# Modulation sums on VectorE earlier, and norm 2 turned into matmul operands in another order

## The chip, the cores and the metric

One core of a Trainium2 chip. The metric is the device time of one execution in microseconds. The kernel of before took 2047.05 us (median of three runs, 2043.01 to 2047.86). One more execution was profiled; it took 2050.43 us, of which the profile's span, from the first to the last instruction, is 2048.7 us.

## The reference, cut to what matters

One layer of a diffusion backbone, on 128 context and 128 latent tokens of width 2048, all in float32. A conditioning vector per stream gives six modulation vectors of width 2048; the layer is a mixer and a feed-forward:

```python
mod = silu(c) @ w_mod + b_mod          # 2048 -> 6 * 2048, once for c_ctx and once for c
shift1, scale1, gate1, shift2, scale2, gate2 = split(mod, 6)
h = rmsnorm(x, norm1_g) * (1 + scale1) + shift1
...                                    # h @ w_in, three branches, their projections
x = x + gate1 * (merged @ w_out)
h2 = rmsnorm(x, norm2_g) * (1 + scale2) + shift2
x = x + gate2 * (square(relu(h2 @ w_ff1)) @ w_ff2)
```

The output is a last rmsnorm of x, and the final states of two of the branches.

## The kernel before

**Tiles.** All weights are stored as tiles of 128 x 1024 floats (0.52 MB), called units here. For each unit SP issues a load into a buffer raw; ScalarE rounds it to wh (type fp32r); VectorE subtracts and leaves the rest in wl. The activations are kept in the same two parts: Hh and Hl hold 16 k-tiles of 128 features by 256 tokens. A product of two such numbers is three matmuls: high with high, low weight with high, high weight with low activation. So most units are 24 matmuls of 256 columns or 12 of 512.

**Order.** The program is one list of steps, 674 units long, that run_stream walks in order; it splits up to three units (two more from a second set of buffers in the first part) ahead of the matmuls. All other work (norms, scans, residuals) are generators, the fillers: pump, called between matmuls, lets them add instructions to the engines' queues as long as a planned clock says that VectorE and ScalarE are not too far ahead of TensorE. A filler that must be done is forced by finish. Each engine executes its queue in the order in which this planner wrote it.

**Modulation.** shift1 and scale1 are made on TensorE at the start. gate1, shift2, scale2 and gate2 (chunks 2 to 5) are made on VectorE by mods, the background filler, which is last in the list and runs only when VectorE's planned time is under 0.8 us ahead of TensorE's. A chunk is 32 pieces. A piece is one 128 x 1024 tile of w_mod, loaded into mraw by SP two pieces ahead, and two VectorE instructions that multiply it with the broadcast vector cb (one for each stream) and sum the products into part. quota says from which unit on piece m may run, so that the sums are spread: gate1, shift2 and scale2 are pieces 0 to 95, gate2 is 96 to 127 and waits until the first feed-forward block is through. The marks a to e are unit numbers:

```python
if m < 72:
    return a + (b - a) * m / 72
if m < 96:
    return b + (c - b) * (m - 72) / 24
return d + (e - d) * (m - 96) / 32
```

a is unit 88, b unit 370 (the start of the two last branch projections, 16 units), c is six units before the end of the output projection (unit 412 of 418), d and e lie in the feed-forward.

**Output projection.** 32 units in four parts: 16 for the left half of the columns (part 0), 8 for the next quarter (1), and twice 4 for an eighth each (2 and 3). After each part resid multiplies the result in PSUM with gate1, adds it to x (both on VectorE), and ScalarE squares and sums it. At the start of part 3 stands

```python
call(lambda: (self.drain_mod(3), self.drain_mod(4), self.make_gs(1, 0, 16), ...))
```

where drain_mod forces the background until the chunk is done, and make_gs forms (1 + scale2) * norm2_g.

**Norm 2.** x lies with tokens on the partitions. norm2(0) finishes the residuals, computes 1/rms of each token (rtok) and starts eight generators modulate2, one for each pair of k-tiles: VectorE scales x by 1/rms into a temporary tp, TensorE transposes it into a PSUM bank pf, ScalarE writes scale * pf + shift to Hh, VectorE writes the same in full precision over pf, and subtracts Hh from it to make Hl. The pair that comes first (one=True) does this one k-tile after the other. Each pair is finished one unit before the feed-forward's first block, ff1(0, 0), reads it. There block takes the k-tiles in order; within a k-tile each of the eight column groups gets its three products (high, low weight, low activation) one behind the other, and pump is called after every second group.

Of the kernel before, what the change touches and what calls it, by code (L numbers as in the profile page):

```python
# [7 lines left out]
F32 = mybir.dt.float32  # L8
F32R = mybir.dt.float32r
U8 = mybir.dt.uint8  # L10
AF = mybir.ActivationFunctionType
ALU = mybir.AluOpType
AX = mybir.AxisListType

P = 128
# [16 lines left out]
W = "wait"  # L32
# [162 lines left out]
class Backbone:  # L195
# [255 lines left out]
            elif s["kind"] == "call":  # L451
                s["do"]()

    def block(self, units, nk, xh, xl, evac, orient="B", pre=None):


        nc = self.nc
        st = {}
        steps = []
        per = nk // len(units)  # L460
        cols = NB // per
        nb = max(4 // per, 1)

        def do(u, hi, lo):
            if u == 0:
                if pre is not None:
                    pre()
                st["b"] = [self.psb.tile([P, 512], F32, tag="b", name=self.nm("pb")) for _ in range(nb)]
            if u >= len(units) - 2:
                self.evac = self.t["pe"] + 24 * 0.12 * (len(units) - u)  # L470
            for k in range(u * per, u * per + per):
                off = (k - u * per) * cols
                ah, al = xh(k), xl(k)
                for c in range(2 * cols // min(cols, 512) if orient == "A" else 2 * nb):
                    if orient == "B":
                        o = st["b"][c // 2][:, (c % 2) * 256:(c % 2) * 256 + 256]
                        w = slice(off + c * P, off + c * P + P)
                        ops = ((hi[:, w], ah), (lo[:, w], ah), (hi[:, w], al))
                        first, lastc = c % 2 == 0, c % 2 == 1
                    else:  # L480
                        n = min(cols, 512)
                        z, v = divmod(c * n, cols)
                        o = st["b"][c * n // 512][:, c * n % 512:c * n % 512 + n]
                        w = slice(off + v, off + v + n)
                        t = slice(z * P, z * P + P)
                        ops = ((ah[:, t], hi[:, w]), (ah[:, t], lo[:, w]), (al[:, t], hi[:, w]))
                        first, lastc = c * n % 512 == 0, (c + 1) * n % 512 == 0
                    for j, (a, b) in enumerate(ops):
                        nc.tensor.matmul(o, lhsT=a, rhs=b, start=(k == 0 and j == 0 and first),
                                         stop=(k == nk - 1 and j == 2 and lastc), skip_group_check=True)  # L490
                    if lastc:
                        self.pump()
            if u == len(units) - 1:
                self.evac = np.inf
                evac(st["b"])

        for u in range(len(units)):
            steps.append(dict(kind="mm", unit=units[u], do=lambda hi, lo, u=u: do(u, hi, lo)))
        return steps
# [223 lines left out]
    def quota(self, m):  # L723

        a, b, c, d, e = self.marks
        if m < 72:
            return a + (b - a) * m / 72
        if m < 96:
            return b + (c - b) * (m - 72) / 24
        return d + (e - d) * (m - 96) / 32  # L730

    def mods(self, chs):
# [657 lines left out]
    def run(self):  # L1390
        nc, I = self.nc, self.I
# [4 lines left out]
        hh = lambda k: self.Hh[:, k, :]  # L1396
        hl = lambda k: self.Hl[:, k, :]
# [8 lines left out]
        def win(blk, **kw):  # L1406
            return self.block([I["win"][blk, k] for k in range(16)], 16, hh, hl, **kw)
# [18 lines left out]
        def call(f):  # L1426
            return [dict(kind="call", do=f)]
# [3 lines left out]
        steps = self.start_steps(win(1, evac=act_evac("FF", 1, AF.Sigmoid)),  # L1431
                                 self.block(half(0), 16, hh, hl, act_evac("FB", 2, AF.Sigmoid)))
        A = win(3, evac=act_evac("qA", 3, AF.Silu))
        B = self.block(half(1), 16, hh, hl, act_evac("FB", 2, AF.Sigmoid, 2))
# [4 lines left out]
        count = lambda: sum("unit" in s for s in steps)  # L1439
        marks = [count()]  # L1440
# [16 lines left out]
        for part in range(3):  # L1457
            pre, evac = self.qkv_evac(part)
# [125 lines left out]
        for part, (c, i, c0, _) in enumerate(PIECES):  # L1584
            w = I["wout" + c]
            wo = self.block([w[part - 2 if c == "c" else 0, k] for k in range(w.shape[1])], 16, hh, hl,
                            lambda b, part=part: resid(b, part), orient="A",
                            pre=(lambda: self.finish(*self.resids)) if c == "c" else None)
# [29 lines left out]
        def ff1(g, blk):  # L1618
            def pre():
                if (g, blk - 1) in self.hidgen:  # L1620
                    self.finish(self.hidgen[g, blk - 1])
                if blk == 0:
                    z = (8, 9, 10, 11) if g % 2 == 0 else (0, 1, 2, 3)
                    self.hid[g] = [self.slot(i, [P, 8, 256], F32R) for i in z]

            def square(r):
                hi, lo = self.hid[g][blk], self.hid[g][2 + blk]
                for j in range(4):
                    nc.vector.tensor_tensor(out=r[:, j, :], in0=r[:, j, :], in1=r[:, j, :], op=ALU.mult)
                yield W  # L1630
                for j in range(4):
                    nc.scalar.copy(flat(hi, j), r[:, j, :])
                yield W
                for j in range(4):
                    nc.vector.tensor_tensor(out=flat(lo, j), in0=r[:, j, :], in1=flat(hi, j).bitcast(F32), op=ALU.subtract)

            def evac(b):
                r = self.slot(4 if blk == 0 else 7, [P, 4, 512])
                for j in range(4):
                    nc.scalar.activation(r[:, j, :], b[j], AF.Relu)  # L1640
                self.hidgen[g, blk] = self.add(square(r), first=True)

            steps = self.block([I["wff1"][2 * g + blk, k] for k in range(16)], 16, hh, hl, evac, pre=pre)
            if g == 0 and blk == 0:
                out = [dict(kind="call", do=lambda: norm2(0), hold=True)]
                for k, s in enumerate(steps):
                    out += [s]
                    if k % 2 == 0 and k // 2 + 1 < 8:
                        out += call(lambda c=k // 2 + 1: norm2(c))
                return out  # L1650
            return steps
# [53 lines left out]
            self.fing = self.slot(10, [P, D])  # L1705
            nc.gpsimd.dma_start(self.fing, I["fing"].partition_broadcast(P))

        marks += [count() - 6, count() + 16, count() + 160]
        self.marks = marks
        f1 = ff1(0, 0) + call(lambda: setattr(self, "late", True)) + ff1(0, 1) + ff1(1, 0) + ff1(1, 1)  # L1710
        steps += f1
        steps += ff2(0, 0) + ff2(0, 1) + ff1(2, 0) + ff1(2, 1) + ff2(1, 0) + ff2(1, 1)
# [8 lines left out]
        for s in range(2):  # L1721
            v, f = self.x1[1][:, s, 768:1024], self.fing[:, 1792:2048]
            nc.vector.scalar_tensor_tensor(out=v, in0=v, scalar=r[:, s:s + 1], in1=f, op0=ALU.mult, op1=ALU.mult)
            for i, c, w, dve in ((0, 0, 512, False), (0, 512, 512, True), (1, 0, 768, s == 1)):
                v = self.x1[i][:, s, c:c + w]
# [46 lines left out]
    def modulate2(self, n0, x, r, one=False):  # L1772


        nc = self.nc
        k, h = yield from self.gettmp()
        h2 = h.rearrange("p (a b) -> p a b", a=2)
        i = None
        for js in ((0,), (1,)) if one else ((0, 1),):
            c, n = js[0] * P, len(js) * P  # L1780
            for s in range(2):
                nc.vector.tensor_scalar(out=h[:, 256 * s + c:256 * s + c + n], in0=x[:, s, c:c + n], scalar1=r[:, s:s + 1], scalar2=None, op0=ALU.mult)
            yield W
            if i is None:
                i, b = yield from self.getbank()
            for j in js:
                for s in range(2):
                    nc.tensor.transpose(b[:, 256 * j + s * P:256 * j + s * P + P], h[:, 256 * s + j * P:256 * s + j * P + P], self.ident)
            yield W
            o = [(self.Hh[:, n0 + j, s * P:s * P + P], b[:, 256 * j + s * P:256 * j + s * P + P],  # L1790
                  self.gs[:, 1, n0 + j, s:s + 1], self.modc[:, 3, n0 + j, s:s + 1]) for j in js for s in range(2)]
            for d, v, g, sh in o:
                nc.scalar.activation(d, v, AF.Identity, bias=sh, scale=g)
            for m, (d, v, g, sh) in enumerate(o):
                j, s = js[m // 2], m % 2
                nc.vector.tensor_scalar(out=v, in0=v, scalar1=g, scalar2=sh, op0=ALU.mult, op1=ALU.add)
            yield W
            j = js[0]
            hi, lo = self.Hh[:, n0 + j:n0 + j + len(js), :], self.Hl[:, n0 + j:n0 + j + len(js), :]
            nc.vector.tensor_tensor(out=lo, in0=b[:, 256 * j:256 * j + 256 * len(js)].rearrange("p (a b) -> p a b", a=len(js)),  # L1800
                                    in1=hi.bitcast(F32), op=ALU.subtract)
        self.putbank(i)
        self.puttmp(k)

# [95 lines left out]
```

## Time and profile before

| what | value |
|---|---|
| median of three runs | 2047.05 us |
| profiled execution | 2050.43 us, span 2048.7 us |
| TensorE matmul busy | 1958.6 us, 96% of the span |
| VectorE busy | 1484.5 us, 72% |
| ScalarE busy | 1013.3 us, 49% |
| of VectorE: splits wl | 610 x 1221 ns, 741.6 us |
| of VectorE: modulation sums junk<-mraw,cb | 256 x 1219 ns, 312.2 us |
| loads of mraw | 128 x 512 KB on SP's queue |
| HBM traffic | 224 GB/s over the span |

All rows of the profile bear one line, L171, since a helper records every instruction; so the tiles' names tell the work. pb is a PSUM bank of the main matmuls, pf one of the fillers', wh and wl are the split weights, Hh and Hl the split activations, mraw and junk the modulation sums, tp a temporary, z a large buffer with many uses, modc the modulation vectors, rtv, rtu and rtr the steps of 1/rms. A row gives an engine, an operation, out<-in with shapes, and in brackets the idle time before it and what ended it. The windows' PEclk is the granted TensorE clock, 1.00 being full.

### The profile page before, as it was taken

The numbers are of one execution on the slowest core, as the hardware profiler recorded it, in microseconds if no ns is written. First come the engines' busy times: TensorE is split into PE (matmuls) and PEld (weight loads), VectorE is DVE, ScalarE is ACT, GpSimd is POOL, SyncE is SP. The second block draws the span as 40 slices with busy tenths as digits, with TensorE's granted clock in tenths as the row PEclk, the third lists the DMA queues.
The fourth block names the chain that finished last, engine by engine and source line by source line (L and its number), as shares of the span: only waits on it lengthen the run. The fifth ranks groups of instructions, "written<-read, shape, count | busy, mean of one in ns | idle before, by whom it ended". The sixth has DMA issues, their size and how long they took to land.

```text
span 2048.7 us, 31030 instructions
## 1 busy us (share of the span) xinstructions
PE 1958.6 (96%) x12023; PEld 1727.4 (84%) x12023; DVE 1484.5 (72%) x2128; ACT 1013.3 (49%) x1486; POOL 49.1 (2%) x120
## 2 busy tenths in 40 slices
PE   5999999999999999999999997699999999999997
PEld 3769988999888889888888876599988998998886
DVE  6875797978887998556876878766676676555475
ACT  6774645476645544366434433444444443344343
POOL 0000000000000000110000000000000000000000
PEclk9999999999999999999999998799999999999998
DMA  9876665655567757655687777466667667566663
GB/s 339 312 288 216 206 206 195 217 192 184 178 206 232 261 195 246 216 185 194 232 301 252 256 279 253 158 202 222 225 228 254 217 227 237 191 201 210 208 235 136
DMA packets 124508, 460.55 MB, mean 225 GB/s; under 512 B 14216, under 2 KB 14792, under 8 KB 122184
## 3 DMA queue, kind: packets, MB, share of 16 engines
q1 hardware_dynamic: 116496, 423.96, 61.0%
q0 software_dynamic: 7568, 34.35, 4.9%
q8 instruction: 94, 1.54, 0.3%
q14 instruction: 54, 0.44, 0.1%
q10 hardware_dynamic: 296, 0.26, 0.0%
HBM read 447.97 MB, written 10.53 MB: 224 GB/s over the span
## 4 chain that ended last, share of the span: by engine, by line
PE 56%; DVE 9%; DMA 4%; ACT 2%; issue 2%; POOL 0%; DVEq 0%; ACTq 0%; SPq 0%; POOLq 0%
PE pb L171 53%; PE pf L171 4%; DVE wl L171 3%; DVE z L171 2%; DVE junk L171 1%; DVE m L171 1%; ACT wh L171 1%; DMA raw<-in_win 1%; DMA z<-in_s0gd 1%; DMA raw<-in_wouta 1%; DMA raw<-in_woutb 1%; DMA raw<-in_woutc 0%; DVE pf L171 0%; DMA mraw<-in_wmodr 0%; ACT L171 0%
## 5 line engine op out<-in xcount | busy, mean ns | idle before, releaser
L171 DVE TENSOR_TENSOR wl<-raw,wh 128x1024 fp32r<-128x1024 f32 x610 | 741.6, 1221 | 471.6 <-ACT wh L171 470.9
L171 ACT CAST wh<-raw 128x1024 fp32r<-128x1024 f32 x610 | 637.1, 1048 | 828.4 <-PE pb L171 686.3
L171 PE MATMUL pb<-Hh,wh 128*128 128x256 f32 x1864 | 533.4, 286 | 5.5 <-ACT Hh L171 3.1
L171 PE MATMUL pb<-Hl,wh 128*128 128x256 f32 x1864 | 529.8, 284 | 1.1 <-DVE Hl L171 1.1
L171 PE MATMUL pb<-Hh,wl 128*128 128x256 f32 x1864 | 529.6, 284 | 0.2 <-DVE wl L171 0.2
L171 PE MATMUL pb<-wh,z 128*128 128x512 f32 (+1 forms) x1472 | 444.2, 383 | 3.3 <-ACT z L171 3.3
L171 PEld LDWEIGHTS pb<-Hh,wh 128*128 128x128 f32 x1864 | 358.6, 192 | 8.1 <-ACT Hh L171 3.3
L171 PEld LDWEIGHTS pb<-Hl,wh 128*128 128x128 f32 x1864 | 358.4, 192 | 1.6 <-DVE Hl L171 1.5
L171 PEld LDWEIGHTS pb<-Hh,wl 128*128 128x128 f32 x1864 | 358.7, 192 | 1.1 <-DVE wl L171 0.4
L171 PE MATMUL pb<-wh,Hh 128*128 128x512 f32 (+1 forms) x800 | 317.0, 396 | 24.8 <-ACT wh L171 22.8
L171 PEld LDWEIGHTS pb<-wh,z 128*128 128x128 f32 x1472 | 273.2, 189 | 59.5 <-ACT z L171 4.5
L171 DVE SCALAR_TENSOR_TENSOR junk<-mraw,cb 128x1024 bf16<-128x1024 f32 x256 | 312.2, 1219 | 4.7 <-DMA mraw<-in_wmodr 2.4
L171 PE MATMUL pb<-wl,Hh 128*128 128x512 f32 (+1 forms) x800 | 307.0, 384 | 3.4 <-DVE wl L171 3.4
L171 PE MATMUL pb<-wh,Hl 128*128 128x512 f32 (+1 forms) x800 | 306.4, 383 | 0.0
L171 PE MATMUL pb<-wl,z 128*128 128x512 f32 (+1 forms) x736 | 281.8, 383 | 0.9 <-DVE wl L171 0.9
L171 PEld LDWEIGHTS pb<-wh,Hh 128*128 128x128 f32 x800 | 151.9, 190 | 53.5 <-ACT wh L171 23.7
L171 PEld LDWEIGHTS pb<-wl,Hh 128*128 128x128 f32 x800 | 151.9, 190 | 30.6 <-DVE wl L171 5.3
L171 PEld LDWEIGHTS pb<-wh,Hl 128*128 128x128 f32 x800 | 151.5, 189 | 29.7
L171 PEld LDWEIGHTS pb<-wl,z 128*128 128x128 f32 x736 | 138.5, 188 | 28.8 <-DVE wl L171 1.1
L171 DVE TENSOR_TENSOR z<-z,z 128x512 f32<-128x512 f32 (+4 forms) x120 | 90.8, 788 | 13.2 <-ACT z L171 9.4
L171 DVE SCALAR_TENSOR_TENSOR cy<-z,par,cy 128x258 f32<-128x258 f32 (+1 forms) x192 | 53.7, 332 | 1.9
L171 PEld LDWEIGHTS pf<-m,z 128*128 128x128 f32 x384 | 49.7, 191 | 3.7 <-ACT z L171 0.4
(187 smaller groups left out, 1366.0 us busy)
## 6 DMA issues: line engine op xcount, KB each, us to landing
raw<-in_win SPq DMA_DIRECT2D x249, 512.0 KB, 4.0
raw<-in_wff SPq DMA_DIRECT2D x224, 512.0 KB, 4.3
mraw<-in_wmodr SPq DMA_DIRECT2D x128, 512.0 KB, 5.4
raw<-in_wbr SPq DMA_DIRECT2D x48, 512.0 KB, 4.2
z<-in_wmods SPq DMA_DIRECT2D x39, 512.0 KB, 5.6
raw<-in_wmods SPq DMA_DIRECT2D x25, 512.0 KB, 6.3
cb<-csd POOLq DMA_DIRECT2D x8, 1024.0 KB, 7.7
raw<-in_wouta SPq DMA_DIRECT2D x16, 512.0 KB, 4.5
```

What stands on the lines that cost most here:

```text
L171: return f(*a, **k)
```

## The change

Three edits. (1) In quota 84 pieces instead of 72 are due by b, and the other 12 by c, which is now 24 units before the end of the output projection (unit 394) instead of six. (2) In modulate2 all scalings come first, then all transposes into one bank, then the rest for each k-tile; this holds for the first pair too, which had one chain behind the other. VectorE's full-precision result goes to the temporary instead of back into PSUM, and the subtraction reads it there; the wait before the subtraction falls away for the first pair. (3) In ff1(0, 0) alone (late=True) block issues, for each k-tile, the 16 products with Hh of all eight column groups first, and the 8 with Hl behind them; pump is called among the last 8.

```diff
-    def block(self, units, nk, xh, xl, evac, orient="B", pre=None):
+    def block(self, units, nk, xh, xl, evac, orient="B", pre=None, late=False):
...
+                for c in range(8 if late else 0):
+                    o = st["b"][c // 2][:, (c % 2) * 256:(c % 2) * 256 + 256]
+                    for m, w in enumerate((hi, lo)):
+                        nc.tensor.matmul(o, lhsT=w[:, c * P:c * P + P], rhs=ah, start=(k == 0 and m == 0 and c % 2 == 0),
+                                         stop=False, skip_group_check=True)
...
                     for j, (a, b) in enumerate(ops):
+                        if late and j < 2:
+                            continue
...
-        if m < 72:
-            return a + (b - a) * m / 72
+        if m < 84:
+            return a + (b - a) * m / 84
         if m < 96:
-            return b + (c - b) * (m - 72) / 24
+            return b + (c - b) * (m - 84) / 12
...
-            steps = self.block([I["wff1"][2 * g + blk, k] for k in range(16)], 16, hh, hl, evac, pre=pre)
+            steps = self.block([I["wff1"][2 * g + blk, k] for k in range(16)], 16, hh, hl, evac, pre=pre, late=(g, blk) == (0, 0))
...
-        marks += [count() - 6, count() + 16, count() + 160]
+        marks += [count() - 24, count() + 16, count() + 160]
...
-        for js in ((0,), (1,)) if one else ((0, 1),):
+        parts = ((0,), (1,)) if one else ((0, 1),)
+        for js in parts:
             c, n = js[0] * P, len(js) * P
             for s in range(2):
                 nc.vector.tensor_scalar(out=h[:, 256 * s + c:256 * s + c + n], in0=x[:, s, c:c + n], scalar1=r[:, s:s + 1], scalar2=None, op0=ALU.mult)
-            yield W
-            if i is None:
-                i, b = yield from self.getbank()
+        yield W
+        i, b = yield from self.getbank()
+        for js in parts:
             for j in js:
                 for s in range(2):
                     nc.tensor.transpose(b[:, 256 * j + s * P:256 * j + s * P + P], h[:, 256 * s + j * P:256 * s + j * P + P], self.ident)
-            yield W
...
-            for d, v, g, sh in o:
-                nc.scalar.activation(d, v, AF.Identity, bias=sh, scale=g)
-            for m, (d, v, g, sh) in enumerate(o):
-                j, s = js[m // 2], m % 2
-                nc.vector.tensor_scalar(out=v, in0=v, scalar1=g, scalar2=sh, op0=ALU.mult, op1=ALU.add)
-            yield W
+        yield W
+        for js in parts:
+            o = [(j, s, b[:, 256 * j + s * P:256 * j + s * P + P], self.gs[:, 1, n0 + j, s:s + 1], self.modc[:, 3, n0 + j, s:s + 1])
+                 for j in js for s in range(2)]
+            for j, s, v, g, sh in o:
+                nc.scalar.activation(self.Hh[:, n0 + j, s * P:s * P + P], v, AF.Identity, bias=sh, scale=g)
+            for j, s, v, g, sh in o:
+                nc.vector.tensor_scalar(out=h2[:, j, s * P:s * P + P], in0=v, scalar1=g, scalar2=sh, op0=ALU.mult, op1=ALU.add)
+            if not one:
+                yield W
...
-            nc.vector.tensor_tensor(out=lo, in0=b[:, 256 * j:256 * j + 256 * len(js)].rearrange("p (a b) -> p a b", a=len(js)),
-                                    in1=hi.bitcast(F32), op=ALU.subtract)
+            nc.vector.tensor_tensor(out=lo, in0=h2[:, j:j + len(js), :], in1=hi.bitcast(F32), op=ALU.subtract)
```

More of the change, by code (lines that the diff above doesn't have):

```diff
@@ L1788, in modulate2 @@
                     nc.tensor.transpose(b[:, 256 * j + s * P:256 * j + s * P + P], h[:, 256 * s + j * P:256 * s + j * P + P], self.ident)
-            yield W
-            o = [(self.Hh[:, n0 + j, s * P:s * P + P], b[:, 256 * j + s * P:256 * j + s * P + P],
-                  self.gs[:, 1, n0 + j, s:s + 1], self.modc[:, 3, n0 + j, s:s + 1]) for j in js for s in range(2)]
-            for d, v, g, sh in o:
-                nc.scalar.activation(d, v, AF.Identity, bias=sh, scale=g)
-            for m, (d, v, g, sh) in enumerate(o):
-                j, s = js[m // 2], m % 2
-                nc.vector.tensor_scalar(out=v, in0=v, scalar1=g, scalar2=sh, op0=ALU.mult, op1=ALU.add)
-            yield W
+        yield W
[8 more added lines that the diff above has]
+                yield W
             j = js[0]
             hi, lo = self.Hh[:, n0 + j:n0 + j + len(js), :], self.Hl[:, n0 + j:n0 + j + len(js), :]
-            nc.vector.tensor_tensor(out=lo, in0=b[:, 256 * j:256 * j + 256 * len(js)].rearrange("p (a b) -> p a b", a=len(js)),
-                                    in1=hi.bitcast(F32), op=ALU.subtract)
+            nc.vector.tensor_tensor(out=lo, in0=h2[:, j:j + len(js), :], in1=hi.bitcast(F32), op=ALU.subtract)
         self.putbank(i)
```

## The prediction

> **What bounds the kernel now.** The page comes first: its span, the TensorE row, and TensorE's share and clock in 40 slices of 51.2 us.
>
> ```profile
> span 2048.7 us, 31030 instructions
> PE 1958.6 (96%) x12023; PEld 1727.4 (84%) x12023; DVE 1484.5 (72%) x2128; ACT 1013.3 (49%) x1486; POOL 49.1 (2%) x120
> ...
> PE   5999999999999999999999997699999999999997
> ...
> PEclk9999999999999999999999998799999999999998
> ```
>
> TensorE is busy all through; besides the ends, only slices 24 and 25 (from 1229 us) have a hole, and the clock falls there. That is the end of the output projection, and norm 2. The waits of TensorE from 1240 to 1345 us (total, times, longest), then the time line of the hole:
>
> ```profile
> PE pb L171 <- ACT wh L171: 22.8, 1, 22.8
> PE pf L171 <- DVE tp L171: 8.3, 4, 4.2
> ...
> PE pb L171 <- DVE Hl L171: 1.1, 1, 1.1
> ```
>
> ```profile
> 1260.85 1.22 DVE L171 SCALAR_TENSOR_TENSOR junk<-mraw,cb 128x1024 bf16<-128x1024 f32 x1
> ...
> 1261.34 22.24 SPq L171 DMA_DIRECT2D mraw<-in_wmodr  x9
> ...
> 1268.05 1.22 DVE L171 SCALAR_TENSOR_TENSOR junk<-mraw,cb 128x1024 bf16<-128x1024 f32 x1 [2.18 <-DMA mraw<-in_wmodr]
> ...
> 1285.78 0.19 DVE L171 TENSOR_TENSOR modc<-part,modc 128x32 f32<-128x32 f32 x1
> ...
> 1287.03 0.42 ACT L171 ACTIVATE junk<-z 128x256 bf16<-128x256 f32 x1 [25.84 <-DVE z L171]
> ...
> 1288.30 2.92 ACT L171 CAST wh<-raw 128x1024 fp32r<-128x1024 f32 x3
> ...
> 1289.38 0.58 PE L171 MATMUL pb<-wh,Hh 128*128 128x256 f32 x1 [22.84 <-ACT wh L171]
> ```
>
> The wait named after ScalarE is VectorE's. At part 3 of the output projection drain_mod(4) forces all sums that are still due into VectorE's queue, from 1260.85 to 1285.78 us. Behind them stand part 2's residual adds; ScalarE's squares wait 25.84 us for these; in ScalarE's queue the cast of the fourth and last weight tile stands behind the squares. TensorE had three tiles ready, ran dry at 1289.38 - 22.84 = 1266.54 us, and had that one tile left. How many sums were left? Windows of the instructions that touch mraw alone (x counts two rows for a sum, two sums for a piece, so x/4 pieces), then the same stretches for all engines:
>
> ```profile
> core 0: us, DVE busy (x), PEclk, DMA share, GB/s
> 819.20:1125.50 306.30, 60.08 (x98) 1.00 0.68 230
> 1125.50:1197.00 71.50, 19.60 (x32) 1.00 0.74 249
> 1197.00:1257.00 60.00, 15.85 (x25) 1.00 0.80 283
> 1257.00:1260.80 3.80, 1.35 (x4) 1.00 0.91 280
> 1260.80:1286.00 25.20, 22.17 (x36) 0.68 0.69 236
> ```
>
> ```profile
> core 0: us, PE busy (x) PEld busy (x) DVE busy (x) ACT busy (x) POOL busy (x), PEclk, DMA share, GB/s
> 819.20:1125.50 306.30, 300.37 (x1547) 254.05 (x1546) 207.41 (x278) 156.13 (x285) 19.21 (x49) 1.00 0.68 230
> 1125.50:1197.00 71.50, 71.48 (x326) 58.31 (x325) 62.41 (x82) 31.39 (x36) 2.11 (x4) 1.00 0.74 249
> 1197.00:1257.00 60.00, 58.07 (x294) 48.79 (x293) 46.57 (x57) 25.91 (x33) 0.54 (x1) 1.00 0.80 283
> ```
>
> 36/4 = 9 pieces were drained, so 87 of 96 were done: about 1 from 1257.0, 6 and 8 in the two stretches before, hence 72 at 1125.5 us, the start of the last branch projection. That is just the 72 which quota() allows there: until then the quota sets the pace, not VectorE. Afterwards it is behind (all 96 were allowed by unit 412 of 418).
>
> **The change part by part.**
>
> (1) *Quota.* 84 instead of 72 by unit 370, 96 by unit 394 instead of 412. A piece costs VectorE two sums. From 1260.85 us to 1285.78 us nine pieces took 24.93 us, 2.18 of them waiting for a load, so 2.53 us a piece. Twelve pieces move ahead of 1125.5 us: 30.4 us of VectorE, into stretches with room (819 to 1125 us: 306.30 - 207.41 = 98.9 us idle). After 1125.5 us the planner got 15 pieces in before the drain with a quota that ran ahead of it; now 12 are needed. So I take none to be left at part 3. In the last stretch there are fewer: about 9 fit by unit 394 at the old rate, 3 remain after it, where 6 or 7 ran.
>
> Without a drain, TensorE goes on at 1266.54 us with the last tile's 24 matmuls. Their spacing at full clock comes from one more row of the windows of all engines, 16.00/135 = 0.1185 us; then the time line of the norm:
>
> ```profile
> 1336.00:1352.00 16.00, 16.00 (x135) 16.00 (x135) 7.80 (x7) 5.36 (x6) 0.00 (x0) 1.00 0.59 196
> ```
>
> ```profile
> 1295.02 0.42 DVE L171 TENSOR_TENSOR z<-pb,z 128x256 f32<-128x256 f32 x1 [2.17 <-PE pb L171]
> ...
> 1298.75 0.48 DVE L171 TENSOR_SCALAR tp<-z,rtr 128x128 f32<-128x128 f32 x2
> ...
> 1299.19 0.66 PE L171 MATMUL pf<-ident,tp 128*128 128x128 f32 x2 [4.20 <-DVE tp L171]
> 1299.89 0.81 ACT L171 ACTIVATE Hh<-pf,modc,gs 128x128 fp32r<-128x128 f32 x2 [1.95 <-PE pf L171]
> 1300.73 0.87 DVE L171 TENSOR_SCALAR pf<-pf,gs,modc 128x128 f32<-128x128 f32 x2 [1.49 <-ACT Hh L171]
> ...
> 1302.31 0.69 PE L171 MATMUL pf<-ident,tp 128*128 128x128 f32 x2 [2.46 <-DVE tp L171]
> ...
> 1302.65 0.56 PE L171 MATMUL pb<-Hh,wh 128*128 128x256 f32 x1
> ```
>
> 24 x 0.1185 = 2.84 us and 0.2 for the last one to end: the residual add of 1295.02 us starts at 1269.6 us. **Term: -25.4 us.** Part 2's adds (1.7 us) then run while TensorE works on the three tiles. The loads that the nine pieces made SP issue in a row (22.24 us) go with the drain; the moved pieces issue as many, two pieces ahead, on the same SP queue as the weights, each holding it until a sum frees its buffer. DMA is at 0.68 of its time in the stretch that takes most: 12 x 0.52 MB over 306 us add 20 GB/s to 230, some 0.06.
>
> What do the moved sums cost where they go? TensorE's idle time from 819 to 1125 us is 306.30 - 300.37 = 5.9 us with VectorE at 207.4. If it grows as VectorE's work does, 5.9 x 30.4/207.4 = 0.9 us. Bounds: 0 (from 1125 to 1197 us VectorE is 87% busy and TensorE idles 0.02 us) and the whole 30.4 us. I take the proportional value, being nearest to that measured stretch. **Term: +0.9.**
>
> (2) *Two tiles turned together.* Before, the first pair's chain runs twice in front of the first matmul of the feed-forward (1302.65 us): transposes at 1299.19, then at 1302.31 us. Now there are four scalings (0.48/2 = 0.24 us each: done by about 1299.7), four transposes (the last two 0.14 us later, until about 1300.3), two activations (0.81), and the first matmul can start near 1301.2 us. **Term: -1.4 us**, between 0 (if it still waits for all four activations and the scalings between them: 0.81 + 0.87 us more) and -2.0 (transposes as fast as the first two). The second k-tile's chain hides behind the first tile's 24 matmuls (2.84 us or more). VectorE's output goes to the temporary instead of PSUM at the same count and sizes; for the subtraction these rows from the whole run bound the gain to nothing:
>
> ```profile
> L171 DVE TENSOR_TENSOR Hl<-pf,Hh 128x512 fp32r<-128x512 f32 x15 | 10.0, 684 | 0.1
> ...
> L171 DVE TENSOR_TENSOR Hl<-tp,Hh 128x512 fp32r<-128x512 f32 x8 | 5.5, 686 | 1.0 <-ACT Hh L171 1.0
> ```
>
> (3) *Low-part products last*, in ff1(0,0) only: same matmuls and weight loads. Hl is asked for at the 17th matmul of a unit instead of the third, 14 x 0.1185 = 1.7 us later, more than the 1.1 us that TensorE waited for it. **Term: -1.1**, between 0 and -1.1. Behind a matmul that waits for Hl stand the later pairs' transposes, and the planner now inserts fillers only after the 18th matmul of a unit. The waits for tp other than the 4.2 and 2.46 us sum to 8.3 - 6.7 = 1.6 us; they may go, or come again for each of seven pairs at the same 0.8 us each (5.6): -1.6 to +4. I take 0, since pairs are finished a unit ahead of their use.
>
> (4) *Clock.* Windows around norm 2:
>
> ```profile
> 1293.68:1297.10 3.42, 1.30 (x11) 1.10 (x10) 1.61 (x4) 0.82 (x3) 0.11 (x1) 1.00 0.81 281
> 1297.10:1300.51 3.41, 0.66 (x2) 0.32 (x2) 1.46 (x8) 1.02 (x5) 0.95 (x2) 0.50 0.81 267
> ...
> 1303.92:1307.34 3.42, 3.42 (x18) 3.42 (x18) 3.35 (x8) 0.85 (x1) 0.00 (x0) 0.50 0.02 5
> ```
>
> A window 38% busy (1.30 of 3.42) was followed by half clock, and the first tile of ff1 ran at 3.42/18 = 0.19 us a matmul. The 4.2 us of resid, norm and scaling stay, so I expect half clock there again: 0. The Trainium skill ("TensorE: Matmul & The Clock Gate", What's actually happening) halves the clock after an idle window of about 3.4 us; read strictly, an idle time of 4.2 us holds a whole free-running window in only about one case in four, and the clock would mostly stay full. The 38% window speaks against the strict reading.
>
> **Sum**: -25.4 + 0.9 - 1.4 - 1.1 = -27.0 us. The profiled execution took 2050.43 us (its span and 1.73 around it), so 2023.4; the median of the runs lies 3.4 lower at 2047.05, which gives **2020 us**.
>
> **Rivals.**
>
> *Some pieces stay.* After the drain 3.6 us pass until TensorE goes on, and it had work until 1266.54 us, so 2.1 us of drain are free and each piece more costs 2.53. Three left: 3 x 2.53 - 2.1 = 5.5, or **2025.5 us**. For it: VectorE's 87%. Against: 15 fitted where 12 are needed.
>
> *The clock stays full at norm 2.* 24 x (0.19 - 0.1185) = 1.7 us and 0.3 on transposes: **2018 us**.
>
> *The quota doesn't do what it says*: VectorE has no room that the planner accepts, and nine pieces are drained as before. Only (2) and (3) remain: **2044.5 us**. Against: the exact 72 at unit 370.
>
> *Slower: the moved sums push the weight splits out one for one*, in the branch projections and the first half of the output projection, where a tile's TensorE work of about 2.8 us meets a split and a sum on VectorE. 12 pieces cross unit 370 and some 3 more crowd before unit 394: 15 x 2.53 = 38, so 2020 - 0.9 + 38 = **2057 us**. It decides from about 11 pieces fully exposed (27.9 us). Against: 98.9 us of room, and 0.02 us of idle TensorE at 87%.
>
> **How the numbers follow.** Forecast 0.68 (own range 2015 to 2024), pieces that stay 0.15, full clock 0.10, no effect 0.04, slower 0.03. About 0.3% (6.1 us) is what a measurement of this kernel can tell from no change: faster 0.93, same 0.04, slower 0.03. The range 2012 to 2030 holds the first three, with the waits for tp both ways and the 4.8 us over which the runs of before spread.
>
> **What would show it.** In the changed profile: no SP row of many mraw loads near part 3; no wait of TensorE of over 3 us for wh between 1200 and 1300 us; 84 pieces summed when the last branch projection starts; TensorE's waits for tp of 4.2 us once, without the 2.46; no wait for Hl; still half clock there. Slices 24 and 25 should stand at 8 or 9. A long run of sums at part 3, or TensorE's idle time from 819 to 1257 us growing by more than 5 us, would make the prediction wrong.

## The result, and the profile after

The changed kernel takes 2011.65 us (median of four runs, 2007.39 to 2015.45) against 2046.92 us for the kernel before: a ratio of 0.9831, 95% interval 0.9804 to 0.9858, or 35.3 us less. The forecast was 2020 us with a range of 2012 to 2030. The direction and the main cause were right; the gain is 8 us larger than forecast, and the median lies 0.35 us below the range. The profiled execution took 2014.46 us. The runs of one kernel spread with their granted clock: those of the changed kernel took 2007.39 us at a mean clock of 0.991, 2008.85 at 0.990, 2014.46 at 0.988 and 2015.45 at 0.987. From the page after: span, instructions, TensorE's busy share and its granted clock in 40 slices.

```profile
span 2012.7 us, 31034 instructions
PE 1954.7 (97%) x12023; PEld 1728.0 (86%) x12023; DVE 1480.8 (74%) x2128; ACT 1014.3 (50%) x1487; POOL 49.0 (2%) x120
...
PE   5999999999999999999999999899999999999997
...
PEclk9999999999989999999999999999999999999998
```

Slices 24 and 25 stand at 9 and 8 where they stood at 7 and 6. To see where 36.0 us of span went, both traces are cut at the same events: the cast of weight tile 55 (counted from 0), the last matmul of the output projection before and behind the hole, the first matmul of the feed-forward, the cast of weight tile 420, the end. Windows of all engines, before (seven stretches; the third is the hole, the fourth the tile left behind it, the fifth norm 2, the sixth the first feed-forward block), then after (no hole; the third is norm 2):

```profile
core 0: us, PE busy (x) PEld busy (x) DVE busy (x) ACT busy (x) POOL busy (x), PEclk, DMA share, GB/s
0.00:178.50 178.50, 151.79 (x903) 108.81 (x904) 122.18 (x142) 121.62 (x161) 3.03 (x9) 0.94 0.81 293
178.50:1266.54 1088.04, 1071.42 (x6362) 945.58 (x6360) 857.51 (x1369) 563.38 (x930) 40.26 (x100) 1.00 0.66 224
1266.54:1289.38 22.84, 0.01 (x2) 0.00 (x1) 19.17 (x35) 2.01 (x6) 0.00 (x0) 0.57 0.52 174
1289.38:1294.98 5.60, 4.92 (x24) 4.43 (x24) 3.47 (x3) 1.84 (x2) 0.00 (x0) 0.62 0.59 181
1294.98:1302.65 7.67, 1.00 (x6) 0.65 (x5) 4.72 (x17) 2.03 (x7) 1.06 (x2) 0.64 0.79 278
1302.65:1410.00 107.35, 104.60 (x849) 103.48 (x849) 77.46 (x115) 54.27 (x80) 0.00 (x0) 0.98 0.56 187
1410.00:2048.70 638.70, 624.82 (x3889) 564.46 (x3887) 400.02 (x450) 268.15 (x303) 4.77 (x9) 0.99 0.64 214
```

```profile
0.00:174.17 174.17, 147.28 (x903) 105.81 (x904) 121.96 (x142) 121.40 (x161) 3.02 (x9) 0.97 0.83 300
174.17:1264.43 1090.26, 1078.11 (x6385) 953.84 (x6384) 879.12 (x1406) 568.64 (x938) 40.12 (x100) 0.99 0.67 228
1264.43:1270.62 6.19, 1.09 (x5) 0.69 (x5) 3.47 (x15) 2.03 (x7) 1.06 (x2) 0.81 0.86 265
1270.62:1373.98 103.36, 103.36 (x847) 103.23 (x848) 76.46 (x118) 54.11 (x80) 0.00 (x0) 0.98 0.60 199
1373.98:2012.70 638.72, 624.81 (x3889) 564.44 (x3887) 399.75 (x450) 268.17 (x303) 4.76 (x9) 0.99 0.63 214
```

| stretch | before | after | difference | forecast |
|---|---|---|---|---|
| start | 178.50 | 174.17 | -4.3 | 0 |
| middle: branches, output projection, without the drain's cost | 1091.1 | 1090.3 | -0.8 | +0.9 |
| the drain: hole 22.84, and 2.6 more for its last tile at half clock | 25.4 | 0 | -25.4 | -25.4 |
| norm 2 | 7.67 | 6.19 | -1.5 | -1.4 |
| first feed-forward block | 107.35 | 103.36 | -4.0 | -1.1 |
| rest | 638.70 | 638.72 | 0 | 0 |
| sum | | | -36.0 | -27.0 |

The 2.6 are the 5.60 us of the fourth stretch less the 2.84 + 0.2 us which the same 24 matmuls need at full clock; 1088.04 + 5.60 - 2.6 = 1091.1. Three readings need care. The start is no part of the change: up to 206.7 us both traces issue the same instructions, and over all the kernels of this study that stretch took 172.2 to 178.5 us, with the old quota or the new. The first row of each table above shows where the 4.3 us lie: the granted clock is 0.94 before and 0.97 after, and TensorE is busy for 151.79 and 147.28 us with the same 903 matmuls. The middle of one execution varies too (1085.9 to 1090.5 us among nine kernels with the new quota), in part for the same reason: TensorE is busy there for 1078.11 us in this profile but for 1075.54 in that of the run *no_late* below, since the clock was at half for 20.5 us of the middle here and for 13.7 there. So -0.8 is one draw from a spread; below it is taken over all kernels. And the block gained more than any step of the prediction gave it.

The waits of TensorE from 1210 to 1330 us, after (total, times, longest), and the time line there:

```profile
PE pf L171 <- DVE tp L171: 4.2, 1, 4.2
PE pb L171 <- ACT Hh L171: 0.9, 1, 0.9
```

```profile
1264.47 0.42 DVE L171 TENSOR_TENSOR z<-pb,z 128x256 f32<-128x256 f32 x1 [0.57 <-PE pb L171]
...
1268.20 0.87 DVE L171 TENSOR_SCALAR tp<-z,rtr 128x128 f32<-128x128 f32 x4
1268.63 1.09 PE L171 MATMUL pf<-ident,tp 128*128 128x128 f32 x4 [4.20 <-DVE tp L171]
1269.76 0.81 ACT L171 ACTIVATE Hh<-pf,modc,gs 128x128 fp32r<-128x128 f32 x2 [2.38 <-PE pf L171]
...
1270.62 0.58 PE L171 MATMUL pb<-Hh,wh 128*128 128x256 f32 x1 [0.90 <-ACT Hh L171]
```

The 22.8 us for wh, the second chain's 2.46 us and the 1.1 us for Hl are gone. Four scalings stand together, then four transposes, then two activations; the feed-forward starts 1.99 us after the transposes did (1268.63 to 1270.62), where the old chain took 3.46 us (1299.19 to 1302.65). SP no longer issues modulation tiles in a row: its time line has the feed-forward's weights there.

```profile
1252.41 36.96 SPq L171 DMA_DIRECT2D raw<-in_wff  x10
```

Windows of the sums alone (x/4 pieces): 83 pieces were done at the last branch projection, 10 more followed until 1200 us and 3 until 1256 us, and none ran at part 3.

```profile
178.50:1117.90 939.40, 203.64 (x332) 0.99 0.66 226
1117.90:1200.00 82.10, 24.51 (x40) 1.00 0.75 261
1200.00:1256.00 56.00, 7.36 (x12) 1.00 0.72 240
1256.00:1285.00 29.00, 0.00 (x0) 0.88 0.59 195
```

### The profile page after: what moved, and what is told of

It is laid out like the page before. It is cut to its first block, busy times and chain, and to the rows that moved or that the text cites. A ratio compares the mean times of both kernels' runs of the same rounds, so it can differ in the third digit from the quotient of the medians.

```text
span 2012.7 us, 31034 instructions
## 1 busy us (share of the span) xinstructions
PE 1954.7 (97%) x12023; PEld 1728.0 (86%) x12023; DVE 1480.8 (74%) x2128; ACT 1014.3 (50%) x1487; POOL 49.0 (2%) x120
## 4 chain that ended last, share of the span: by engine, by line
PE 85%; DVE 6%; DMA 4%; ACT 2%; issue 2%; SPq 0%; DVEq 0%; POOL 0%; ACTq 0%; POOLq 0%
PE pb L171 76%; PE pf L171 9%; DVE wl L171 2%; DVE z L171 1%; ACT wh L171 1%; DVE m L171 1%; DMA raw<-in_win 1%; DVE junk L171 1%; DMA raw<-in_wmods 1%; DMA z<-in_s0gd 0%; DMA raw<-in_winh 0%; DMA z<-in_winh 0%; ACT tp L171 0%; ACT z L171 0%; DMA cb<-csd 0%
## 5 line engine op out<-in xcount | busy, mean ns | idle before, releaser
L171 PE MATMUL pb<-Hl,wh 128*128 128x256 f32 x1864 | 513.1, 285 | 0.2 <-DVE Hl L171 0.2
L171 PEld LDWEIGHTS pb<-Hl,wh 128*128 128x128 f32 x1864 | 351.5, 193 | 0.5 <-DVE Hl L171 0.4
```

What stands on the lines that cost most here:

```text
L171: return f(*a, **k)
```

## The experiments

The edits are called (1) quota, (2) turn, (3) late, as in the prediction.

### One part alone, and two of three

*Quota alone*: the kernel before with edit (1). *Turn and late alone*: the changed kernel with the old quota.

```diff
# quota_only, against before
-        if m < 72:
-            return a + (b - a) * m / 72
+        if m < 84:
+            return a + (b - a) * m / 84
...
-        marks += [count() - 6, count() + 16, count() + 160]
+        marks += [count() - 24, count() + 16, count() + 160]
```

> The new quota alone, norm 2 and the first feed-forward block as before. Theory A (the terms of the sum are independent): no wait of TensorE for wh of over 3 us near the end of the output projection, 25.4 us less there, against 0.9 us or less more where the sums go; time 25 us under the kernel before (2022 us beside 2047). The first block keeps its wait for Hl of 1.1 us, the second wait for tp of 2.5 us and the small ones of 1.6 us. Theory B (the 9 us beyond the forecast also come from the sums' new places): 30 us or more under the kernel before, so 2017 us or less. Where the sums cost VectorE time one for one: no faster than before.

> The old quota, with the two tiles turned together and the low-part products last. Theory A: nine pieces still drained, the wait of 22.8 us stays; 1.4 us less before the first matmul of the feed-forward and 3.9 us less within its first block: 5.3 us under the kernel before (2042 us beside 2047). Theory B: 1.4 and 1.1 us as forecast, so 2.5 us under it.

The quota alone took 2016.46 us (ratio 0.9845, 0.9831 to 0.986), the two others alone 2042.51 us (0.9974, 0.996 to 0.9989): -31.1 and -5.0 us against 2047.55, together -36.1, so the parts add up to the whole change. The first is what theory B of its expectation said (30 us or more), the second what theory A said (5.3 us). The waits, of the quota alone and then of turn and late alone:

```profile
PE pf L171 <- DVE tp L171: 8.3, 4, 4.2
PE pb L171 <- DVE Hl L171: 1.0, 1, 1.0
```

```profile
PE pb L171 <- ACT wh L171: 23.8, 1, 23.8
```

With the quota alone the hole is gone and the old waits of norm 2 are all there; without it the hole stands. So the hole is the drain's, and the two other edits are worth 5 us without any help from the first. The forecast of the parts was -24.5 for the quota and -2.5 for turn and late; both are low.

*Turn without late, late without turn*, both with the new quota:

```diff
# no_late, against the changed kernel
-            ... late=(g, blk) == (0, 0))
+            ... late=False)
# no_turn: modulate2 as it was before
```

> The changed kernel without the low-part products last. Theory A (the order of the products is what ended the waits for Hl and for tp in the first feed-forward block): the block is 3.9 us longer again, with a wait for Hl of some 1 us and waits for tp of some 2 us; 2015.5 us beside 2011.6. Theory B (the waits for tp went because VectorE no longer writes over PSUM): only the wait for Hl comes back, 1.1 to 1.3 us.

> The changed kernel with norm 2's chain as before (first pair one k-tile after the other, VectorE writing over PSUM). Theory A: the second wait for tp of about 2.5 us before the first matmul is back, that matmul comes 1.4 us later after the last one of the output projection, and the rest of the first block is as in the changed kernel; 2013 us beside 2011.6. Theory B: also the 2 us of waits for tp within the block are back: 3.5 us more in all.

Without late: 2010.59 us (0.982, 0.9804 to 0.9835). Without turn: 2013.83 us (0.9835, 0.9818 to 0.9852). On the whole time neither can be told from the changed kernel, whose runs spread over 8 us; the stretch of the block can. The waits of the two (no_late, then no_turn), and the windows of their blocks in the same order with that of the quota alone as a third:

```profile
PE pf L171 <- DVE tp L171: 4.2, 1, 4.2
PE pb L171 <- DVE Hl L171: 1.1, 2, 0.7
```

```profile
PE pf L171 <- DVE tp L171: 7.5, 5, 4.2
```

```profile
1264.78:1370.17 105.39, 104.30 (x846) 103.80 (x847) 77.07 (x118) 54.56 (x80) 0.00 (x0) 0.97 0.58 195
```

```profile
1266.62:1372.24 105.62, 104.73 (x848) 103.43 (x848) 77.38 (x115) 54.07 (x80) 0.00 (x0) 0.98 0.58 190
```

```profile
1269.23:1375.73 106.50, 103.82 (x849) 102.63 (x848) 77.47 (x115) 54.35 (x80) 0.00 (x0) 0.99 0.57 189
```

TensorE's idle time in the block is the window less its busy time: 2.75 us before, 2.68 with the quota alone, 0.89 without turn, 1.09 without late, 0.00 with both. Without late the 1.1 us for Hl is there, in two waits; without turn the waits for tp are. So late takes away the wait for Hl and half of those for tp beside the 4.2 and 2.46 us (7.5 - 6.7 = 0.8 are left of 1.6), turn takes away all of these but not the wait for Hl, and only both leave nothing. No run separates late's two parts, the order of the products and the later place of the fillers. The block's length also hangs on how long its first matmuls run at half clock: 4.69 us before, 2.76 with the quota alone, 4.60 without turn, 6.24 without late, 4.49 after. With 0.376 us taken off for each such microsecond (1 - 0.1185/0.19, the prediction's two spacings), the blocks measure 105.6, 105.5, 103.9, 103.05 and 101.7 in that order: turn is worth some 2.5 us in the block, late 1.6, both 3.9. That the correction is sound shows in the eight kernels with turn, late and a half clock in front of the block: they take 102.9 to 104.1 us, and 101.65 to 101.8 with it.

### Where does turn's part of the block come from?

Two things were put into edit (2): the order, and the place to which VectorE writes its full-precision result. The run *psum_out* is the one without late, with the result written over the PSUM bank as before, where the subtraction then reads it:

```diff
-                nc.vector.tensor_scalar(out=h2[:, j, s * P:s * P + P], in0=v, ...
+                nc.vector.tensor_scalar(out=v, in0=v, ...
...
-            nc.vector.tensor_tensor(out=lo, in0=h2[:, ...
+            nc.vector.tensor_tensor(out=lo, in0=b[:, ...
```

> The changed kernel without the low-part products last, and with VectorE writing its full-precision result over PSUM as before instead of to the temporary; the two first tiles are still turned together. To be compared with the kernel that differs in the destination alone (no low-part products last, result to the temporary), whose first block, from its first matmul to the cast of weight tile 420, took 105.39 us, of which 6.23 us at half clock: 103.05 us without what that cost. Theory G (the destination makes VectorE faster: four results in 1.37 us instead of 1.77, 0.40 us a pair, 2.8 us for seven pairs, and this is what ended the waits for tp): four results take 1.77 us again, waits for tp of 1 to 2 us and for Hl of 1 us are back, and the block is about 2.5 us longer, 105.6 us without the half clock's cost. Theory H (the order of the instructions ended them): the block stays at 103 us.

It took 2015.1 us (0.9846, 0.9829 to 0.9864). Groups of instructions by form in the block, VectorE (xcount | busy us, mean ns of one): no_late, then psum_out; then psum_out's waits.

```profile
L171 DVE TENSOR_SCALAR tp<-pf,gs,modc 128x128 f32<-128x128 f32 x32 | 11.0, 404 | 2.5 <-ACT Hh L171 2.5
```

```profile
L171 DVE TENSOR_SCALAR pf<-pf,gs,modc 128x128 f32<-128x128 f32 x32 | 13.3, 417 | 3.4 <-ACT Hh L171 2.6
```

```profile
PE pf L171 <- DVE tp L171: 4.7, 3, 4.2
PE pb L171 <- DVE Hl L171: 1.7, 2, 1.1
```

The mean of one instruction differs by 13 ns, which over 32 would be 0.4 us. But the busy time differs by 2.3 us. To SBUF the 32 rows overlap (32 x 404 ns is 12.9 us, in 11.0 us of busy time), over PSUM they don't (32 x 417 ns is 13.3): back to back, a result written over PSUM keeps the next one waiting longer than its own row tells. A run of four and the instruction behind it show it, in the time lines of psum_out and of no_late:

```profile
1279.34 1.77 DVE L171 TENSOR_SCALAR pf<-pf,gs,modc 128x128 f32<-128x128 f32 x4
1281.03 1.22 DVE L171 TENSOR_TENSOR wl<-raw,wh 128x1024 fp32r<-128x1024 f32 x1
```

```profile
1275.72 1.37 DVE L171 TENSOR_SCALAR tp<-pf,gs,modc 128x128 f32<-128x128 f32 x4
1277.00 1.22 DVE L171 TENSOR_TENSOR wl<-raw,wh 128x1024 fp32r<-128x1024 f32 x1
```

The next instruction starts 1.69 us after the first of the four in psum_out and 1.28 us after it in no_late. 0.40 us for each of seven pairs is 2.8 us of an engine that is on the path here. With the results back in PSUM the waits for Hl grow from 1.1 to 1.7 us, some of those for tp return, and the block takes 106.99 us, 105.15 with the half-clock part taken off, against 103.05 for no_late. So about 2.1 of turn's 2.5 us in the block are the destination, and about 0.4 the order. The subtraction has no part in it: in both runs the instruction behind it starts 0.61 us later (1278.21 to 1278.82 us in psum_out, 1284.22 to 1284.83 in no_late). Whether PSUM as such is the slower destination or the writing over the place just read was not separated. The Trainium skill ("Perfetto Trace Analysis", Optimizing Scalar/DVE Operations) gives VectorE an overhead of about 60 ns an instruction on SBUF and 125 on PSUM, without saying whether the source or the destination counts; an estimate by that page, if the destination does, is 32 x 0.065 = 2.1 us. The rows' busy time, 2.3 us, is close to it; by the starts, 0.41 us for four or 0.10 for one, the difference is larger than the page's 0.065.

### The quota and the mark

```diff
# mark_only: 72 pieces by b, the other 24 by unit 394
-        if m < 84:
-            return a + (b - a) * m / 84
+        if m < 72:
+            return a + (b - a) * m / 72
# due84_mark6: 84 by b, the other 12 by unit 412
-        marks += [count() - 24, ...
+        marks += [count() - 6, ...
```

> The changed kernel with 72 pieces due by unit 370 as before and 24 by unit 394. Theory A (behind unit 370 the planner's room on VectorE sets the pace, not the quota): the same nine pieces or so are drained at part 3, the wait of some 23 us is back; 25 us over the changed kernel. Theory C (the earlier mark lets more run): fewer than five pieces drained, under 12 us over it.

> The changed kernel with 84 pieces due by unit 370 and the last 12 by unit 412, as late as before. Theory A: 12 pieces in 42 units is slower than the 15 that fitted, so none or one is drained; within 2 us of the changed kernel at the place of the drain. Theory C (the mark 24 units ahead matters): several pieces drained, 2.5 us for each over it.

Both runs have turn and late. With the earlier mark but not the 84 (mark_only) the kernel took 2042.27 us (0.9976, 0.9963 to 0.9988), as with neither (norm_only, 2042.51); with the 84 but not the earlier mark 2013.07 us (0.9832, 0.9817 to 0.9846), about as with both (2011.65). With mark_only TensorE waits nearly as long as before, and the window of the sums alone shows nine pieces (x36) drained:

```profile
PE pb L171 <- ACT wh L171: 21.6, 1, 21.6
```

```profile
1262.00:1290.00 28.00, 22.18 (x36) 0.71 0.64 216
```

Permission is not capacity. Allowed to run earlier, the sums did not: from the last branch projection on VectorE has no more room that the planner accepts. Only pieces moved ahead of that stage are gained, and the mark does nothing measurable. mark_only lies 31 us above the changed kernel where 25 were expected; some 5 more are the gain of the moved sums (below).

### What a piece that stays behind costs

```diff
     def quota(self, m):
+        if 95 <= m < 96:      # keep1;  keep5: 91 <= m < 96
+            return 10 ** 6
```

The held pieces are forced at part 3.

> The changed kernel with its last piece of scale2 held back until part 3 forces it. Theory A (a drained piece costs TensorE 2.53 us beyond about 2.1 us that are free): 0.4 us more at that place, at most 1; within the spread of the runs.

> The changed kernel with its last five pieces of scale2 held back until part 3 forces them. Theory A: 5 x 2.53 - 2.1 = 10.6 us of TensorE's time, up to 2.2 more if a load is late: one wait for wh of 10 to 13 us, and 10 to 13 us over the changed kernel. Rival (what makes the hole is not the count of sums, but that anything is forced there): the wait is 20 us or more, or under 3.

keep5 took 2025.38 us (0.9888, 0.9873 to 0.9903), keep1 2013.19 us (0.983, 0.9814 to 0.9847). TensorE's wait at part 3, keep5 and then keep1:

```profile
PE pb L171 <- ACT wh L171: 10.8, 1, 10.8
```

```profile
PE pb L171 <- DVE wl L171: 0.9, 1, 0.9
PE pb L171 <- ACT wh L171: 0.2, 1, 0.2
```

Five pieces at 2.53 us and a load wait of 0.87 inside the drain make 13.5 us; 10.8 come through to TensorE, so 2.7 us were free where the prediction had 2.1. One piece costs about 1 us, though by that figure it should cost nothing: the free room is not a hard edge. keep5 as a whole lies 13.7 us above the changed kernel; its last tile also ran at half clock (granted from 1262 to 1276 us), as the tile behind the hole of before did. The rival of pieces that stay had TensorE's wait right within 0.8 us (10.6 and 0.4 by its price, 10.8 and 1.1 measured) and left out the half clock behind a long wait; it just did not happen.

### Keeping the clock full

```diff
+                i, b = self.grab()
+                for _ in range(36):
+                    nc.tensor.transpose(b[:, 0:P], self.ident, self.ident)
+                self.putbank(i)
```

This stands in norm2(0) after the residuals, and adds work whose result nobody reads.

> The changed kernel with 36 transposes of the identity into a spare PSUM bank (about 3.9 us of TensorE, results unused) behind the last matmul of the output projection, while the residual, the norm and the scaling run. If half clock costs what the forecast said (1.7 us on the first unit's 24 matmuls and 0.3 on the transposes), the clock stays full through norm 2, the first unit's 24 matmuls take 2.9 instead of 5 us, and the stage from the last real matmul of the output projection to the end of the first feed-forward block is some 2 us shorter; time 2 us under the changed kernel, inside the spread of the runs. Rival (VectorE sets the pace in that block): the clock is full, but the 2 us come back as waits for Hh, Hl or tp.

It took 2012.07 us (0.9825, 0.98 to 0.985), the same as the changed kernel. TensorE's time line and the window of the block:

```profile
1268.07 0.39 PE L171 MATMUL pb<-Hh,wh 128*128 128x256 f32 x1 [0.90 <-ACT Hh L171]
```

```profile
1268.07:1370.94 102.87, 101.78 (x846) 101.33 (x847) 76.46 (x118) 54.20 (x80) 0.00 (x0) 1.00 0.59 201
```

The clock is 1.00 all through the block and the first tile takes 3.14 us (1268.07 to 1271.21) instead of 5.1. But 1.09 us of idle time follows, a wait for the next pair's tp, as the rival said: the block is 0.5 us shorter than in the profile of the changed kernel, not 1.7, and norm 2 in front of it 0.26 us (1262.14 to 1268.07), so 0.75 us of the 2 expected. VectorE's pace, not the clock, ends the first tiles. The half clock in front of them is cover for VectorE's work. Behind the block this kernel loses more than that: 641.3 us to the end against 638.7, with 2.5 us of waits for wl against 0.9. So the equal time is not the block's alone.

### What do the moved sums cost?

The nine kernels with the new quota have a middle (cut as in the table, without a hole) of 1085.9 to 1090.5 us, 1087.5 in the mean; TensorE is idle for 10.8 to 12.15 us of it in the eight beside keep5. The three with the old quota and its hole (before, norm_only, mark_only) have 1093.6 to 1096.6, mean 1094.9, less the 2.6 us of the last tile 1092.3, and idle 16.6 to 18.7 us up to the hole. So the twelve moved pieces did not cost 0.9 us; some 5 us were gained. Two runs asked why.

```diff
# all96: all 96 pieces due by b
+        if m < 96:
+            return a + (b - a) * m / 96
# old_pace: the old pace up to piece 48, the rest of the 84 crowded behind
+        if m < 49:
+            return a + (b - a) * m / 72
         if m < 84:
-            return a + (b - a) * m / 84
+            return a + 192 + (b - a - 192) * (m - 49) / 35
```

> The changed kernel with all 96 pieces due by unit 370, so 24 more than before instead of 12 move ahead of the last branch projection. Forecast's term (TensorE's idle time grows as VectorE's work does): 0.9 us more between unit 100 and the end of the output projection than in the changed kernel. Theory D (the sums cost nothing where they go, what counts is that none are left in the output projection, whose idle time is already 0): the same idle time of 11 to 12 us, within 2 us. Theory E (the crowding in the burst near unit 290 grows): 3 us or more there.

> The changed kernel, but pieces 0 to 48 at the pace of before (until unit 280), and the 35 behind them faster, to 84 by unit 370. Theory D (the saving beside the drain is made in the last branch and the output projection): up to unit 280 the idle times of TensorE are those of before, after it those of the changed kernel or better, in the output projection 0; the total of idle time lies 2 to 3 us under before's 17. Theory F (the early sums only reshuffle the planner's order, and the new order as a whole has less idle time): the total lies anywhere between 11 and 17, and no stage of it is like the changed kernel's.

all96 took 2015.85 us (0.9844, 0.9818 to 0.987), old_pace 2016.15 us (0.9844, 0.982 to 0.9867). By the whole time neither can be told from the changed kernel; the rest rests on one profile of each, in both cases the slowest run. Windows of the middle: all96, then old_pace. Then the same stage of the branches, 756 matmuls long, in all96 and after:

```profile
178.26:1271.32 1093.06, 1075.23 (x6386) 953.19 (x6384) 879.98 (x1406) 568.90 (x938) 40.01 (x100) 0.99 0.66 228
825.12:959.41 134.29, 127.49 (x756) 111.40 (x755) 104.69 (x157) 74.05 (x170) 14.45 (x41) 1.00 0.70 237
```

```profile
174.72:1266.95 1092.23, 1075.27 (x6386) 950.51 (x6384) 878.53 (x1406) 567.09 (x937) 40.04 (x100) 0.99 0.67 228
```

```profile
821.49:950.88 129.39, 127.91 (x756) 111.07 (x755) 84.54 (x125) 75.72 (x185) 14.54 (x41) 1.00 0.63 211
```

With twelve more pieces ahead of the last projection the middle takes 1093.1 us, 5.6 more than that mean, and the idle time goes from 12.15 us to 17.8. 5.3 us of that arise in one stage: 6.8 us idle (134.29 - 127.49) where the changed kernel has 1.5, with 20 us more of VectorE's work there (104.69 against 84.54). That is theory E's size. Its cause is argued, not shown: the waits that grew there are named after ScalarE's z (3.7 us, 0.2 in the changed kernel) and loads of z (3.1, against 0.6), none after a sum. old_pace is idle for 17.0 us, about as long as the old quota, though in the output projection it shows none of the 1.75 to 3.25 us that the old quota had there. Its total is therefore not the 2 to 3 us under before's that theory D gave, though the output projection is as D said. So the place of the sums matters beside their number; the planner's whole order may shift with them. Why 84 spread evenly is better than 72 was not settled. A gain in the output projection, where there are then fewer sums, accounts for about 2 of the 5 us; the rest lies in the branches, without one wait that answers for it.

## Why the prediction was right or wrong

**(1) The drain: right.** Its mechanism (sums, then residual adds, squares, cast) and its 25.4 us hold: 22.84 + 2.6 in the pair, and only the kernels with 72 due by b show the hole of over 20 us. The step "So I take none to be left at part 3" holds too, with 83 pieces at the branch projection. Its reason does as well: mark_only shows that it was the 72 which set the count there, not the mark.

**(1) Crowding, +0.9: the sign was wrong.** "If it grows as VectorE's work does" failed. Over nine kernels the middle got some 5 us shorter, in the pair 0.8. The bound "0" should have lain below nothing: TensorE has 16.6 us of idle time in the middle to lose, and a new quota moves it in either direction (10.8 to 12.15 us with the 84, 17.8 in all96). Which waits it takes away stays open.

**(2) Turn, -1.4 in front of the feed-forward: right**, at -1.5; every kernel with the old chain has 7.67 or 7.68 us there, every one with the new at most 6.20.

**(2) "At the same count and sizes": the step that failed in the block.** The rows bounded the gain of the subtraction to nothing, and 685 against 684 ns holds. The gain was in the instruction before it, whose destination changed. It is worth about 2.1 us (measured without late), and no row of before had that form.

**(3) Low-part products last, -1.1: right in what it named.** The wait for Hl is gone, and comes back with no_late at 1.1 us. **Waits for tp, 0:** mis-sized. The 1.6 us besides 4.2 and 2.46 went away, which was the lower bound given. Of the block's 4.0 us, 2.75 are these two waits. The other 1.2 lie in TensorE's busy time, whose ends are modelled; the records do not show where.

**(4) Half clock stays: right**, and of less weight than the rival gave it. Two windows of 3.41 us each in the run without late:

```profile
1257.37:1260.78 3.41, 1.22 (x11) 1.01 (x9) 2.30 (x5) 0.89 (x4) 0.18 (x1) 1.00 0.81 237
1260.78:1264.19 3.41, 1.09 (x4) 0.68 (x4) 1.86 (x10) 0.60 (x4) 0.88 (x2) 0.50 0.94 321
```

A window in which TensorE was busy for 1.22 of 3.41 us was followed by half clock, as the 38% window was before; the clock fell at 1260.78 us, 2.2 us after the last matmul's end. All kernels but warm had half clock at norm 2. The strict reading of the Trainium skill ("TensorE: Matmul & The Clock Gate", What's actually happening), that the window must be idle, does not fit these rows. The rival's 2.0 us (1.7 and 0.3) were the right size for the matmuls (5.1 to 3.14 us on the first tile, 0.26 in front of it), but the prediction had not asked what would be late next.

**The sum.** -27.0 was forecast, -35.3 measured on the medians. The table's -36.0 holds -4.3 of the start, which are not the change's, and only -0.8 of the middle. With the means over the kernels in their place it reads -25.4 - 4.8 - 1.5 - 4.0 = -35.7. Against the forecast, -5.7 are the crowding term and -2.9 the block. The range ended at 2012 because it allowed no gain for the first and none for the destination.

## What to carry to other kernels

Work that a background generator still owes at a forced point is paid in full at TensorE, less a few microseconds of cover; an earlier permission does not help where the planner finds no room, so the due time must be moved ahead of the full stage. When an edit changes where an instruction writes, price that instruction by runs of several back to back, not by its mean duration. When a wait goes away, ask for the next one: at the full clock the first tile took 3.14 us instead of 5.1, and a wait of 1.09 us for VectorE came behind it.

## What the runs showed of the hardware that was not expected

VectorE's 128x128 result from PSUM takes 1.77 us for four when it is written over the same place in PSUM and 1.37 us to SBUF, while the mean durations (417 and 404 ns) hardly differ. The clock was halved after a window of 3.41 us in which TensorE was 36% busy. And the same instructions at the start of the kernel took between 172.2 and 178.5 us from one profiled execution to the next, which is more than most of the terms argued over here. The granted clock goes with it: it was at half for 6.8 us of that stretch in the shortest and for 20.5 us in the longest.
